# Three padding tiles in a decoder layer on one core, so that every large tile starts on a multiple of 512 bytes

## The chip, the cores and the metric

The kernel runs on one core of a Trainium2 chip. The metric is the device time of one execution in microseconds; several executions of the same program give a median. Its profile comes from one more execution, whose span (first to last instruction) and own time are given separately.

## The reference, cut to what matters

One layer of a decoder over 512 positions of width 2048, all in float32:

```
h    = rmsnorm(x) ;  proj = h @ w_in                    # 2048 -> 4608 columns
o_a  = sliding-window attention, 16 heads on 4 kv heads, window 128, q/k normalised, relative bias, sinks
o_b  = stick-breaking attention, 16 heads (scan of log(1 - sigmoid) from the right), strictly causal
x    = x + concat(rmsnorm(o_a), rmsnorm(o_b)) @ w_out   # 2048 -> 2048
h    = rmsnorm(x)
x    = x + square(relu(h @ w_up)) @ w_down              # 2048 -> 8192 -> 2048
```

## The kernel before

**Numbers as pairs.** Every large matrix product is made of three matmuls: each operand is split into a high part (a cast on ScalarE, L89) and a low part (the difference, on VectorE, L90), and high x high, high x low and low x high are added up in one bank of PSUM. So a tile that is needed for a product comes as `hi_...` and `lo_...`, or as `h2h` and `h2l`.

**Stages.** First come the input's transposes and the projections (`ps_kv`, `ps_qa`, `ps_v`, `ps_qk`), with the attention's small matmuls pumped in between: nine groups of 192 matmuls with 512 columns each. Here the moving or the stationary operand is `hT`, the transposed input (pools `big0` and `big1`), the other one a chunk of weights (pool `whl`). Then the two branches go through the output projection (`ps_o`, L114 to L116 in `mm3`): eight groups of 96 matmuls, stationary `ohl` (pools `big0`, `big1`), moving `hi_o` and `lo_o` (pool `whl`).

The up-projection (`ps_u`, L792 to L794) multiplies by a Winograd-like form of a 2 x 2 block product with seven products in place of eight. It runs over 32 groups g of 256 columns, and in each over 8 steps k: 21 matmuls of 256 columns, stationary `hi_u` and `lo_u` (pool `whl`), moving `h2h` and `h2l` of step k. These stay in SBUF for the whole stage, in pools of their own: `h2_0` to `h2_5` on the right side, `h2_6` and `h2_7` on the left. For each pair of steps GpSimd makes four sums of weights (`s_u`, L769, pool `sp`); ScalarE and VectorE split raw weights and sums (L89, L90). The group before is finished meanwhile, piece by piece (`u_finish`), with `al` (L827) as VectorE's last and longest piece, and its results go to DRAM (`ac`).

The down-projection (`ps_d`, L1023 to L1025) has the same seven-product form over 8 chunks and 2 halves: 2688 matmuls of 512 columns, stationary the stored activations `ad` (pool `ab`, on the right), moving `hi_d` and `lo_d` (pool `whl`). GpSimd makes the sums of weights (`T`, L918), VectorE adds each product to sums that stay in SBUF (`U`, `C`, pool `acc`, L962), and the last chunk brings scale, residual (`x2r`, L948) and the store.

**Order.** Each engine works through its instructions in the order in which the program names them. Loads and stores are issued on SP's queue, a few small ones on ScalarE's.

**Where the tiles lie.** Pools are stacked in each partition of SBUF, from the left (low addresses, upwards) and from the right (high addresses, downwards), and each tile is rounded up to 32 bytes. On the left stand 1,024 bytes of scratch, four constants of 32 bytes and the pool `const` with 1,792 bytes, so that `wst` and `whl` begin at 2,944 = 5 x 512 + 384. They take 16,384 and 32,768 bytes. Behind them `sm` has 28 small slots, 896 bytes, so that the next pool begins at 52,992 = 103 x 512 + 256. The right stack begins at 229,344 = 447 x 512 + 480 and goes down. All the larger tiles are multiples of 512 bytes long and keep their pool's remainder:

| pools | side | tiles | bytes past a multiple of 512, before | after |
|---|---|---|---|---|
| `wst`, `whl` | left | weights, raw and split (`hi_...`, `lo_...`) | 384 | 0 |
| `big1`, `big0`; later `h2_6`, `h2_7`, `ew`, `acc`, `x2p` | left | `hT`, `ohl`; `h2` of k = 6, 7; `a`, `ah`, `al`; `U`, `C`; `x2r` | 256 | 0 |
| `once`, `qkp`, `vp`, `wtp`, `wk`; later `h2_0` to `h2_5`, `sp`, `xw`; later `rw`, `t3`, `ab` | right | attention's tiles, `S`; `h2` of k = 0 to 5, `s_u`, `xs`; `st_d`, `T`, `ad` | 480 | 0 |

480 is 32 bytes off a multiple of 64; 384 and 256 are multiples of 128.

Of the kernel before, what the change touches and what calls it, by code (L numbers as in the profile page):

```python
# [12 lines left out]
F32 = mybir.dt.float32  # L13
# [7 lines left out]
P = 128  # L21
# [37 lines left out]
def hymba_layer(ctx: ExitStack, tc: tile.TileContext, x, norm_attn_g, w_in, q_norm_g, k_norm_g,  # L59
# [7 lines left out]
    const = ctx.enter_context(tc.tile_pool(name="const", bufs=1))  # L67
# [3 lines left out]
    sm = ctx.enter_context(tc.tile_pool(name="sm", bufs=4))  # L71
# [3 lines left out]
    odd, even, attn = ExitStack(), ExitStack(), ExitStack()  # L75
    big = {1: odd.enter_context(tc.tile_pool(name="big1", bufs=KD // 2)),
           0: even.enter_context(tc.tile_pool(name="big0", bufs=KD // 2))}
    once = attn.enter_context(tc.tile_pool(name="once", bufs=1, side="right"))
    qkp = attn.enter_context(tc.tile_pool(name="qkp", bufs=7, side="right"))
    vp = attn.enter_context(tc.tile_pool(name="vp", bufs=8, side="right"))  # L80
# [278 lines left out]
        return o  # L359

    oscr = dram.tile([2 * 8, P, T], F32, name="oscr")
    S = [once.tile([P, T], F32, name=f"S{b}") for b in range(2)]

    def finish_o(av, branch, c, keep=False):

        if c == 0:
            nc.scalar.square(out=S[branch], in_=av)
        else:
            sq = wk.tile([P, T], F32, tag="we", name=f"osq{branch}_{c}")
            nc.scalar.square(out=sq, in_=av)  # L370
            nc.gpsimd.tensor_tensor(out=S[branch], in0=S[branch], in1=sq, op=ALU.add)
        if keep:
# [257 lines left out]
    def branch_scale(b):  # L630
        ps = bank(f"rs{b}")
        for t in range(NT):
            nc.tensor.matmul(ps[:, 2 * t:2 * t + 2], S[b][:, t * P:(t + 1) * P], ones2, start=True, stop=True)
        r = const.tile([P, NT], F32, name=f"rb{b}")
# [345 lines left out]
    for cj in range(2 * NC):  # L980
# [10 lines left out]
        for s, (name, ai, _, b, more) in enumerate(D_PRODUCTS):  # L991
# [19 lines left out]
            if not more:  # L1011
                pool, tag = ((pa, "pa"), (pp, "pp"))[b // 2]
# [46 lines left out]
```

## Time and profile before

| | |
|---|---|
| time before, median of 3 runs (lowest, highest) | 2077.21 us (2077.02, 2078.11) |
| the profiled execution: own time, span | 2076.19 us, 2074.5 us |
| granted TensorE clock, mean | 0.996 |
| TensorE matmuls, busy | 2019.0 us, 97% (11652) |
| VectorE, busy | 1678.5 us, 81% |
| GpSimd, busy | 1045.7 us, 50% |
| ScalarE, busy | 1008.1 us, 49% |
| DMA | 350.28 MB, mean 169 GB/s |

In the rows PE is TensorE, PEld its weight load, DVE VectorE, ACT ScalarE, POOL GpSimd and SP the queue of the loads. A matmul's own duration in the trace overlaps with the next one's, because matmuls are pipelined; TensorE's pace is the distance from one matmul's start to the next one's. Idle time is put down to the instruction that ended it ("<-").

### The profile page before, as it was taken

What the parts mean: (1) busy time and instruction counts of PE and PEld (TensorE: products, weight loads), DVE (VectorE), ACT (ScalarE), POOL (GpSimd) and SP (SyncE); (2) the same over time, 40 slices, a digit from 0 to 9 for tenths busy, and PEclk for the clock granted to TensorE, in tenths of its full rate; (3) what the DMA queues carried; (4) which work ended last, traced back from release to release, by engine and by line L of the source; (5) the groups of instructions that cost most, each with busy time, mean ns of one, the idle gap of its engine ahead of it and who ended that gap; (6) DMA issues with size and microseconds to landing.
All of it is one profiled execution on the core that took longest, in us unless ns stands there. A gap on an engine that the chain in (4) does not pass through costs nothing. (4 is left out here: it accounts for less than half of the span.)

```text
span 2074.5 us, 30963 instructions
## 1 busy us (share of the span) xinstructions
PE 2019.0 (97%) x11652; PEld 1722.1 (83%) x11652; DVE 1678.5 (81%) x2038; ACT 1008.1 (49%) x1692; POOL 1045.7 (50%) x904
## 2 busy tenths in 40 slices
PE   8999999999999999999999999998999999999998
PEld 7777777777677889999999999997788888888876
DVE  4468646565775579999999999998889888988999
ACT  6267534544553565555555555554543333333332
POOL 0013322222220137777778787877755555555663
PEclk9999999999999999999999999999999999999999
DMA  6742332223345535656555555658756456456453
GB/s 217 116 133 82 102 96 73 72 92 117 103 140 175 180 109 163 195 186 194 187 188 194 185 196 184 198 183 326 265 208 230 158 206 244 144 204 260 152 187 108
DMA packets 213913, 350.28 MB, mean 169 GB/s; under 512 B 9779, under 2 KB 154372, under 8 KB 206596
## 3 DMA queue, kind: packets, MB, share of 16 engines
q1 hardware_dynamic: 211216, 345.02, 49.1%
q10 hardware_dynamic: 2548, 3.30, 1.4%
q8 instruction: 91, 1.49, 0.3%
q14 instruction: 58, 0.48, 0.1%
HBM read 270.16 MB, written 78.12 MB: 168 GB/s over the span
## 5 line engine op out<-in xcount | busy, mean ns | idle before, releaser
L794 PE MATMUL ps_u<-h2h,lo_u 128*128 128x256 f32 x1792 | 506.7, 283 | 15.7 <-DVE lo_u L90 15.7
L793 PE MATMUL ps_u<-h2l,hi_u 128*128 128x256 f32 x1792 | 506.4, 283 | 2.7 <-DVE h2l L90 2.7
L792 PE MATMUL ps_u<-h2h,hi_u 128*128 128x256 f32 x1792 | 506.3, 283 | 0.6 <-ACT h2h L89 0.6
L769 POOL TENSOR_TENSOR s_u<-st_u 128x256 f32<-128x256 f32 x256 | 254.6, 1015 | 242.3 <-DVE lo_u L90 171.7
L1024 PE MATMUL ps_d<-lo_d,ad 128*128 128x512 f32 x896 | 357.1, 399 | 6.4 <-DVE lo_d L90 6.4
L1023 PE MATMUL ps_d<-hi_d,ad 128*128 128x512 f32 x896 | 356.5, 398 | 6.5 <-DMA ad<-ac 4.9
L794 PEld LDWEIGHTS ps_u<-h2h,lo_u 128*128 128x128 f32 x1792 | 340.1, 190 | 21.9 <-DVE lo_u L90 21.8
L1025 PE MATMUL ps_d<-hi_d,ad 128*128 128x512 f32 x896 | 356.5, 398 | 0.0
L793 PEld LDWEIGHTS ps_u<-h2l,hi_u 128*128 128x128 f32 x1792 | 337.0, 188 | 3.2 <-DVE h2l L90 3.1
L792 PEld LDWEIGHTS ps_u<-h2h,hi_u 128*128 128x128 f32 x1792 | 336.6, 188 | 1.0 <-ACT h2h L89 1.0
L90 DVE TENSOR_TENSOR lo_d<-T,hi_d 128x1024 fp32r<-128x1024 f32 x128 | 244.8, 1924 | 49.4 <-ACT hi_d L89 49.4
L89 ACT CAST hi_u<-s_u 128x512 fp32r<-128x512 f32 x256 | 158.3, 618 | 226.4 <-POOL s_u L769 226.4
L918 POOL TENSOR_TENSOR T<-st_d,T 128x1024 f32<-128x1024 f32 x64 | 162.6, 2543 | 208.9 <-DVE lo_d L90 207.7
L90 DVE TENSOR_TENSOR lo_u<-s_u,hi_u 128x512 fp32r<-128x512 f32 x256 | 248.0, 969 | 8.6 <-ACT hi_u L89 8.4
L89 ACT CAST hi_d<-T 128x1024 fp32r<-128x1024 f32 x128 | 134.3, 1051 | 214.0 <-PE ps_d L1025 196.8
L1024 PEld LDWEIGHTS ps_d<-lo_d,ad 128*128 128x128 f32 x896 | 169.4, 189 | 49.9 <-DVE lo_d L90 8.9
L1023 PEld LDWEIGHTS ps_d<-hi_d,ad 128*128 128x128 f32 x896 | 169.6, 189 | 48.8 <-ACT a L816 4.9
L90 DVE TENSOR_TENSOR lo_u<-st_u,hi_u 128x384 fp32r<-128x384 f32 x256 | 202.3, 790 | 4.6 <-ACT hi_u L89 4.6
L1025 PEld LDWEIGHTS ps_d<-hi_d,ad 128*128 128x128 f32 x896 | 169.6, 189 | 41.1
L90 DVE TENSOR_TENSOR lo_d<-st_d,hi_d 128x1024 fp32r<-128x1024 f32 x96 | 190.1, 1996 | 13.3 <-ACT hi_d L89 13.2
L89 ACT CAST hi_d<-st_d 128x1024 fp32r<-128x1024 f32 x96 | 100.9, 1051 | 163.5 <-PE ps_d L1025 163.5
L769 POOL TENSOR_TENSOR s_u<-s_u,st_u 128x256 f32<-128x256 f32 x128 | 140.5, 1098 | 0.0
(220 smaller groups left out, 3823.6 us busy)
## 6 DMA issues: line engine op xcount, KB each, us to landing
st_u<-in_w_up SPq DMA_DIRECT2D x128, 512.0 KB, 4.4
st_d<-in_w_down SPq DMA_DIRECT2D x64, 1024.0 KB, 6.1
ad<-ac SPq DMA_DIRECT2D x56, 1024.0 KB, 6.4
ac<-ah SPq DMA_DIRECT2D x32, 896.0 KB
ac<-al SPq DMA_DIRECT2D x32, 896.0 KB, 4.8
st_qk<-in_w_in SPq DMA_DIRECT2D x64, 256.0 KB, 3.0
st_o<-in_w_out SPq DMA_DIRECT2D x32, 512.0 KB, 4.2
st_qa<-in_w_in SPq DMA_DIRECT2D x16, 512.0 KB, 3.8
```

The source lines that it names most:

```text
L89: nc.scalar.copy(out=hi, in_=st)
L90: nc.vector.tensor_tensor(out=lo, in0=st, in1=hi.bitcast(F32), op=ALU.subtract)
L769: nc.gpsimd.tensor_tensor(out=o, in0=a, in1=b, op=op)
L792: nc.tensor.matmul(o, wh[:, a], hh[:, b], start=first, stop=False, skip_group_check=True)
L793: nc.tensor.matmul(o, wh[:, a], hl[:, b], start=False, stop=False, skip_group_check=True)
L794: nc.tensor.matmul(o, wl[:, a], hh[:, b], start=False, stop=(k == KP - 1), skip_group_check=True)
L918: nc.gpsimd.tensor_tensor(out=o, in0=raw[cj, a, h], in1=raw[cj, b, h], op=ALU.subtract)
L1023: nc.tensor.matmul(o, al, bh[:, kk], start=first, stop=False, skip_group_check=True)
L1024: nc.tensor.matmul(o, al, bl[:, kk], start=False, stop=False, skip_group_check=True)
L1025: nc.tensor.matmul(o, ar, bh[:, kk], start=False, stop=end, skip_group_check=True)
```

## The change

Three tiles are allocated that nothing writes or reads: 480 bytes at the top of the right stack, in a pool of their own that is opened ahead of the others; 128 bytes at the end of `const`; 128 bytes in `sm`. 2,944 + 128 = 3,072 = 6 x 512; 52,992 + 256 = 53,248 = 104 x 512; 229,344 - 480 = 228,864 = 447 x 512. Everything else is as before.

```
@@ -75,6 +75,8 @@
     odd, even, attn = ExitStack(), ExitStack(), ExitStack()
     big = {1: odd.enter_context(tc.tile_pool(name="big1", bufs=KD // 2)),
            0: even.enter_context(tc.tile_pool(name="big0", bufs=KD // 2))}
+    edge = ctx.enter_context(tc.tile_pool(name="edge", bufs=1, side="right"))
+    edge.tile([P, 120], F32, name="pad_right")
     once = attn.enter_context(tc.tile_pool(name="once", bufs=1, side="right"))
     qkp = attn.enter_context(tc.tile_pool(name="qkp", bufs=7, side="right"))
     vp = attn.enter_context(tc.tile_pool(name="vp", bufs=8, side="right"))
@@ -359,6 +361,8 @@
         return o
 
     oscr = dram.tile([2 * 8, P, T], F32, name="oscr")
+    const.tile([P, 32], F32, name="pad_left")
+    sm.tile([P, 32], F32, tag="pad", bufs=1, name="pad_small")
     S = [once.tile([P, T], F32, name=f"S{b}") for b in range(2)]
```

## Rows read from the trace of the kernel before

**Rows 1.** Busy time of each engine by stage: window, PE, PEld, DVE, ACT, POOL, clock, DMA.

```profile
0.00:748.00 748.00, 728.37 (x3572) 565.72 (x3573) 455.25 (x782) 381.44 (x796) 160.75 (x264) 1.00 0.41 121
748.00:1422.80 674.80, 655.70 (x5394) 648.52 (x5392) 643.14 (x805) 378.47 (x651) 508.62 (x501) 1.00 0.57 185
1427.40:2074.50 647.10, 634.97 (x2688) 507.83 (x2688) 577.92 (x448) 245.96 (x244) 374.01 (x138) 0.99 0.56 206
```

**Rows 2.** Who waited for whom, 800 to 1400 us: us in total, times, longest.

```profile
ACT hi_u L89 <- POOL s_u L769: 208.0, 57, 5.1
POOL s_u L769 <- DVE lo_u L90: 129.6, 58, 3.0
...
PE ps_u L794 <- DVE lo_u L90: 14.3, 29, 0.8
DVE a L818 <- ACT a L816: 14.0, 29, 0.5
DVE lo_u L90 <- ACT hi_u L89: 7.6, 28, 0.3
```

**Rows 3.** Timeline of VectorE in up: start and duration in us.

```profile
1020.18 2.56 DVE L827 TENSOR_TENSOR al<-a,ah 128x1792 fp32r<-128x1792 f32 x1
...
1041.03 2.56 DVE L827 TENSOR_TENSOR al<-a,ah 128x1792 fp32r<-128x1792 f32 x1
```

**Rows 4.** Busy time in the steady part of down, columns as in the first group.

```profile
1500.00:2000.00 500.00, 500.00 (x2135) 401.94 (x2134) 443.44 (x353) 190.42 (x184) 279.02 (x102) 1.00 0.56 207
```

**Rows 5.** Who waited for whom, 1460 to 2020 us, longest in total.

```profile
ACT hi_d L89 <- PE ps_d L1025: 328.5, 192, 1.8
```

**Rows 6.** The chain that ended last, in order of time: start, us, what.

```profile
1458.48 0.50 PE ps_d L1023
...
2001.11 0.25 PE ps_d L1025
...
2030.53 0.50 PE ps_d L1024
```

**Rows 7.** Timeline of TensorE, one group of up: first of k = 0, first and last of k = 6.

```profile
1004.40 0.28 PE L792 MATMUL ps_u<-h2h,hi_u 128*128 128x256 f32 x1
...
1019.52 0.28 PE L792 MATMUL ps_u<-h2h,hi_u 128*128 128x256 f32 x1
...
1021.89 0.28 PE L794 MATMUL ps_u<-h2h,lo_u 128*128 128x256 f32 x1
```

**Rows 8.** Timeline of TensorE in down: two matmuls, 2134 intervals apart.

```profile
1500.04 0.39 PE L1023 MATMUL ps_d<-hi_d,ad 128*128 128x512 f32 x1
...
2000.01 0.40 PE L1024 MATMUL ps_d<-lo_d,ad 128*128 128x512 f32 x1
```

**Rows 9.** Timeline of TensorE in the branch outputs: two matmuls, 122 intervals apart.

```profile
657.07 0.39 PE L115 MATMUL ps_o<-lo_o,ohl 128*128 128x512 f32 x1
...
685.41 0.39 PE L116 MATMUL ps_o<-hi_o,ohl 128*128 128x512 f32 x1
```

**Rows 10.** Timeline of TensorE in the first projections: two matmuls, 155 intervals apart.

```profile
73.09 0.40 PE L114 MATMUL ps_qa<-hT,hi_qa 128*128 128x512 f32 x1
...
109.26 0.40 PE L116 MATMUL ps_qa<-hT,lo_qa 128*128 128x512 f32 x1
```

**Rows 11.** Instructions of single tiles: duration in ns, min/median/max, first and last start.

```profile
L827 DVE TENSOR_TENSOR al<-a,ah x32: 2024/2559/2565, 793.0 to 1438.4; 128x1792 fp32r<-128x1792 f32 x32
L90 DVE TENSOR_TENSOR h2l<-hq,h2h x8: 2025/2026/2336, 691.4 to 771.4; 128x1792 fp32r<-128x1792 f32 x8
L371 POOL TENSOR_TENSOR S<-S,osq x14: 1273/1289/1296, 193.9 to 640.6; 128x512 f32<-128x512 f32 x14
L973 POOL TENSOR_TENSOR C<-C,U x12: 1286/1745/2282, 2010.7 to 2061.5; 128x512 f32<-128x512 f32 x12
```

**Rows 12.** DMA issues: count, KB each, median us to landing.

```profile
x2r<-x2scr SPq DMA_DIRECT2D x16, 256.0 KB, 3.2
xs<-in_x SPq DMA_DIRECT2D x16, 256.0 KB, 3.1
```

More of the change, by code (lines that the diff above doesn't have):

```diff
@@ L77, in hymba_layer @@
            0: even.enter_context(tc.tile_pool(name="big0", bufs=KD // 2))}
+    edge = ctx.enter_context(tc.tile_pool(name="edge", bufs=1, side="right"))
+    edge.tile([P, 120], F32, name="pad_right")
     once = attn.enter_context(tc.tile_pool(name="once", bufs=1, side="right"))
@@ L361, in hymba_layer @@
     oscr = dram.tile([2 * 8, P, T], F32, name="oscr")
+    const.tile([P, 32], F32, name="pad_left")
+    sm.tile([P, 32], F32, tag="pad", bufs=1, name="pad_small")
     S = [once.tile([P, T], F32, name=f"S{b}") for b in range(2)]
```

## The prediction

> **What bounds the kernel now.** I read the page, then the stages, then who waits for whom in each, and last the starts of single matmuls. The profiled execution took 2076.19 us around its span of 2074.5; the median of the runs shown, 2077.21, is 1.0 above it, so the sum below is made against the profiled execution and carried over to the median as a difference. TensorE is busy 97% of the span, so the first question is in which stage its pace is the time. [rows 1] cuts the span into everything up to the branch outputs, the up-projection ("up") and the down-projection ("down").
>
> In up, 674.8 us, TensorE is busy 655.7 and VectorE 643.1 [rows 1], and the waits between 800 and 1400 us decide [rows 2]: ScalarE waits for GpSimd, GpSimd for VectorE, VectorE a little for ScalarE, nobody for TensorE. TensorE itself waits for VectorE's `lo_u`, 14.3 us in 29 groups, 0.5 us a group. The period shows it, too: `al` starts at 1020.18 and at 1041.03, 20.85 us apart [rows 3]. So up runs at VectorE's period, and TensorE has half a microsecond a group to spare.
>
> Down is the other way round. From 1500 to 2000 us TensorE is busy all of 500.00 us and VectorE 443.44 [rows 4], and between 1460 and 2020 ScalarE alone waits 328.5 us for TensorE, the top line of that view, in which TensorE waits for nobody [rows 5]. The chain that ended last is matmuls from 1458.48 to 2001.11, mostly VectorE up to 2030.53, then both in turn [rows 6]. At least 543 us of down thus go at TensorE's own pace.
>
> **What TensorE's pace is.** Here the starts are to be compared with the offsets of the tiles in the table further up.
> - Up, one group [rows 7]. The moving operand is `h2` of step k. For k = 0 to 5 it lies 480 bytes past a multiple of 512: 126 intervals from 1004.40 to 1019.52, 120.0 ns each. For k = 6, 256 bytes past: 20 intervals from there to 1021.89, 118.5 to 119. This group stands for 29, the fourth on, in which the starts give 120.03 and 118.89. The stationary operand and the neighbours are the same, and the granted clock of up is 1.00 [rows 1], the 2.4 GHz level; the step comes where k goes from 5 to 6. That is 1% for a moving operand at 480.
> - Down [rows 8]: stationary operand at 480, moving at 384. 2134 intervals between matmuls of 512 columns from 1500.04 to 2000.01, 234.29 ns each.
> - Branch outputs [rows 9], with the same roles: stationary `ohl` at 256, moving `hi_o` and `lo_o` at 384. 122 intervals from 657.07 to 685.41, 232.30 ns.
> - First projections [rows 10]: moving `hT` at 256, stationary at 384. 155 intervals from 73.09 to 109.26, 233.35 ns. Before up I found stretches of both paces, 232.3 and 233.4; 234.29 stands in down alone.
>
> So the trace has a price for an operand at 480, which is 32 bytes off a multiple of 64, where 256 and 384 are on one: 1.1 ns for a matmul of 256 columns, 0.9 to 2.0 for one of 512.
>
> **The change part by part.** The three tiles are neither written nor read: no instruction, DMA or wait of theirs is added, and no queue's order changes. What moves is addresses.
> - *Down, the stationary operand from 480 to 0.* In 543 us at 234.29 ns stand 2316 matmuls. Nearest row: the branch outputs, for the same roles. 2316 x (234.29 - 232.30) = 4.6 us gained; with the pace of [rows 10] 2316 x 0.94 = 2.2; if it isn't the offset, 0. I take 4.6, because the roles are the same and the step in up speaks for the offset. VectorE then has 443.4 us of work in 496 and stays under.
> - *Up, the moving operand from 480 to 0.* 126 x 1.14 = 0.14 us a group that TensorE comes earlier to its stop; there it waits 0.14 us longer for `lo_u`, as the period is VectorE's. Cost 0. If that cover were gone (VectorE much quicker), 32 x 0.14 = 4.6 us would be gained.
> - *Everything before up: from 256 and 384 to 0.* By the loops these are 2496 matmuls of 512 columns (nine projection groups of 192 and eight output groups of 96). No row shows an operand at a multiple of 512. 232.30 and 233.35 both occur already; I take 0, with a bound of 2496 x 1.05 = 2.6 us either way, and wider ones among the rivals.
> - *VectorE and GpSimd,* which set up's period. Their quickest instructions are equal at 256 and at 480 [rows 11]: 1792 columns on VectorE take 2024 ns (`al`, 256) and 2025 (`h2l`, six of eight at 480), 512 columns on GpSimd 1286 (`C`, 256) and 1273 (`S`, 480). ScalarE's casts I put at 0 with them. The bound is that 1% of GpSimd's or VectorE's share of up were moved: no more than 674.8 x 0.01 = 6.7 us, and 0.05% by VectorE's rows, 0.3 us. I take 0.
> - *DMAs.* 256 KB land in 3.2 us at 256 (`x2r`) and in 3.1 at 480 (`xs`) [rows 12], and neither in up nor in the steady part of down does TensorE wait for one [rows 2, 5]. 0; should `ad` land later than now, down would stop at the start of a product, which it doesn't do today.
> - *Reuse of space.* The left pools go up by 128 or 256 bytes and the right ones down by 480, so `xw` touches one tile more of `big0`, and `ew` and `acc` one more of `xw`. All of these had their last use before the new pool was opened. 0; a wait that came in all the same would stand once, ahead of the first tile of the pool.
>
> The Trainium skill ("SBUF — State Buffer", section "SBUF: two separate sides") has a rule that speaks against the change: SBUF's cachelines are 16 bytes. Every tile starts on a multiple of 32 already, so by that rule the padding would gain nothing and the time stay at 2077.2, against 2072.6 by the rows. The step in up doesn't agree with it [rows 7].
>
> Sum: -4.6 in down, 0 elsewhere. Profiled execution 2076.2 - 4.6 = 2071.6; median 2077.2 - 4.6 = **2072.6 us**, 0.22% faster.
>
> **The rivals.**
> 1. *Down settles at the slower of the two paces,* 233.35: -2.2, **2075**. For it: [rows 10] holds that pace for 155 matmuls with nothing at 480. Against it: the roles there are exchanged.
> 2. *The offset isn't the cause.* k = 0 to 5 differ from 6 and 7 in the stack, too (right and left), and `ad` is and stays on the right. Then nothing happens: **2077**. Against it: k = 0 to 5 lie all over the right stack and go at one pace.
> 3. *Every step up to 512 counts,* so that 256 and 384 are slow as well. At 1.99 ns an operand: 2 x 1.99 x 2496 = 9.9 us before up, 4.6 for the moving operand in down, 4.6 as above: -19.1, **2058**; half of it is 2067.6. Against it: 256 and 384 exchange their roles between [rows 9] and [rows 10], and no pace belongs to one of them.
> 4. *Slower: both operands at one offset get in each other's way.* Today moving and stationary differ by 96 or 128 bytes modulo 512; afterwards by 0. Priced by the one step that the trace has, 1% or 2.3 ns of 512 columns, in the 2496 matmuls before up: +5.7 us with nothing gained in down, **2083**; in down as well, 2316 x 2.3 = 5.3 more. It decides from 4.6 us / 2496 = 1.8 ns a matmul. Up would not notice: 168 x 1.1 = 0.2 us a group of the 0.5 spare. Nothing in the trace speaks for it or against it, as no pair of operands lies at one offset.
>
> **How the numbers follow.** Forecast 0.42; rivals 0.14, 0.17, 0.13, 0.14. 0.2% is 4.15 us, about what a measurement of this kernel can tell from no change; that line, 2073.05, is close to the forecast. Faster: three quarters of the forecast and all of rival 3, 0.44. Slower: most of rival 4 and a little of rival 2, 0.14. The rest is within 0.2%: 0.42. The forecast's own range is 2070 to 2075. For 8 in 10 it runs from 2063 (three quarters of rival 3) to 2081 (two thirds of rival 4).
>
> **What would show it.** Right: matmuls of down 232.3 ns apart between 1500 and 2000; k = 0 to 5 of up at 118.9 like k = 6, with the wait for `lo_u` 0.14 us longer and `al` still 20.85 apart; paces before up between 232.3 and 233.4; up ending when it did, down some 5 us earlier. Wrong: down still at 234.29 (rival 2), a pace under 232 before up (rival 3) or over 234 there (rival 4), or a period of up that moved, which would mean that VectorE or GpSimd feel the addresses after all.

## The result and the profile after

The changed kernel takes 2051.19 us (median of 4 runs, 2050.44 to 2052.35), the kernel before 2077.66 beside it (4 runs, 2077.02 to 2078.21). The ratio is 0.9873, 95% interval 0.9856 to 0.989: 26.5 us or 1.3% faster. The prediction was 2072.6 us with a range of 2063 to 2081, so the time lies far outside it, on the faster side. The profiled execution took 2051.57 us around a span of 2049.8, 24.7 us under the span before, with the same 30963 instructions and a mean granted clock of 0.995.

First the stages of the changed kernel (window, busy time of PE, PEld, DVE, ACT and POOL, granted clock, DMA share and GB/s); the last row is the steady part of down.

```profile
0.00:740.50 740.50, 720.47 (x3571) 565.63 (x3572) 454.35 (x782) 381.09 (x796) 161.34 (x264) 1.00 0.41 122
740.50:1415.70 675.20, 656.93 (x5394) 650.15 (x5393) 643.70 (x805) 378.61 (x651) 509.10 (x501) 1.00 0.57 185
1420.80:2049.80 629.00, 615.96 (x2688) 506.34 (x2688) 589.60 (x448) 246.51 (x244) 377.33 (x139) 0.99 0.57 211
...
1500.00:1990.00 490.00, 490.00 (x2164) 405.73 (x2163) 460.62 (x359) 191.52 (x183) 288.37 (x106) 1.00 0.55 206
```

Against [rows 1]: everything before up ends at 740.5 instead of 748.0, up lasts 675.2 instead of 674.8, and down with its tail 629.0 instead of 647.1. VectorE's work in up is the same, 643.70 for 643.14. In the steady part of down TensorE is busy without a gap, as in [rows 4], and gets through 2164 matmuls in 490 us where it had 2135 in 500. So 18 us come out of down, 7.5 out of what precedes up, and nothing out of up. No instruction is missing or new; the question is TensorE's pace.

Down, TensorE's timeline of the changed kernel (start and duration in us): two matmuls, 2162 intervals apart.

```profile
1500.17 0.39 PE L1029 MATMUL ps_d<-hi_d,ad 128*128 128x512 f32 x1
...
1990.22 0.39 PE L1028 MATMUL ps_d<-lo_d,ad 128*128 128x512 f32 x1
```

490.05 us / 2162 = 226.67 ns, where [rows 8] give 234.29 and the best pace of [rows 9] was 232.30. At the granted clock of 1.00, which is the 2.4 GHz level, 226.67 ns are 544 cycles, 512 columns and 32 more. The branch outputs have it as well, 120 intervals between these two rows, 226.75 ns each (the first of them are a little longer).

```profile
651.90 0.39 PE L116 MATMUL ps_o<-hi_o,ohl 128*128 128x512 f32 x1
...
679.11 0.39 PE L118 MATMUL ps_o<-hi_o,ohl 128*128 128x512 f32 x1
```

The same steady pace stands in the projections: 226.7 instead of the 232.3 and 233.4 of before. If all 2496 matmuls before up had gained 5.6 ns, that would be 14.0 us, and 7.5 are there. The difference is where the attention's small matmuls are pumped in. After such a block the large matmuls don't have the quick pace at once; here the second `ps_v` after one, and a later one of the same run.

```profile
161.18 0.40 PE L117 MATMUL ps_v<-lo_v,hT 128*128 128x512 f32 x1
161.42 0.40 PE L118 MATMUL ps_v<-hi_v,hT 128*128 128x512 f32 x1
...
162.35 0.39 PE L116 MATMUL ps_v<-hi_v,hT 128*128 128x512 f32 x1
162.58 0.40 PE L117 MATMUL ps_v<-lo_v,hT 128*128 128x512 f32 x1
```

0.24 us from one to the next at first, 0.23 later, and the next block comes soon. Averaged over the whole stretch ahead of up, the second to the eleventh distance after a block are 230.5 ns in the changed kernel, and those from the twelfth on 226.8. Over all intervals under 300 ns from a large matmul to whatever TensorE does next ahead of up (2290 before, 2293 after) the mean falls from 232.6 to 228.8 ns; 2290 x 3.8 = 8.7 us, near the 7.5 by which the stage is shorter.

Up keeps its period, as predicted. Its waits between 800 and 1380 us (us in total, times, longest), to be read beside [rows 2]:

```profile
ACT hi_u L91 <- POOL s_u L773: 203.1, 55, 5.2
POOL s_u L773 <- DVE lo_u L92: 124.9, 56, 3.0
...
PE ps_u L798 <- DVE lo_u L92: 12.7, 28, 0.7
```

TensorE still stops for `lo_u` in every group, 0.45 us a time for 0.49 before (the prediction had this wait grow by 0.14 us), and VectorE's `al` still comes 20.85 us apart, like [rows 3]:

```profile
1013.12 2.56 DVE L831 TENSOR_TENSOR al<-a,ah 128x1792 fp32r<-128x1792 f32 x1
...
1033.97 2.56 DVE L831 TENSOR_TENSOR al<-a,ah 128x1792 fp32r<-128x1792 f32 x1
```

Within a group, though, there is something that the forecast had the other way round. TensorE's timeline of one group in the changed kernel: 124 intervals within k = 0 to 5, then 19 within k = 6.

```profile
997.49 0.28 PE L797 MATMUL ps_u<-h2l,hi_u 128*128 128x256 f32 x1
...
1012.37 0.28 PE L798 MATMUL ps_u<-h2h,lo_u 128*128 128x256 f32 x1
...
1012.61 0.28 PE L797 MATMUL ps_u<-h2l,hi_u 128*128 128x256 f32 x1
...
1014.89 0.28 PE L798 MATMUL ps_u<-h2h,lo_u 128*128 128x256 f32 x1
```

Both stretches go at 120.0 ns. In [rows 7] k = 6 went at 118.9; it has become slower, and k = 0 to 5 no faster. VectorE feels none of it; the quickest `al` and `h2l` take 2024 ns, as in [rows 11] (tile, duration min/median/max in ns, first and last start):

```profile
L831 DVE TENSOR_TENSOR al<-a,ah x32: 2024/2561/2567, 785.9 to 1431.8; 128x1792 fp32r<-128x1792 f32 x32
...
L92 DVE TENSOR_TENSOR h2l<-hq,h2h x8: 2024/2026/2420, 685.1 to 764.2; 128x1792 fp32r<-128x1792 f32 x8
```

### The profile page after: what moved, and what is told of

Read it like the earlier page. It is cut to its first block, busy times and chain, and to the rows that moved or that the text cites. A ratio compares the mean times of both kernels' runs of the same rounds, so it can differ in the third digit from the quotient of the medians.

```text
span 2049.8 us, 30963 instructions
## 1 busy us (share of the span) xinstructions
PE 1993.6 (97%) x11652; PEld 1722.2 (84%) x11652; DVE 1690.3 (82%) x2038; ACT 1008.6 (49%) x1692; POOL 1050.0 (51%) x904
## 5 line engine op out<-in xcount | busy, mean ns | idle before, releaser
L798 PEld LDWEIGHTS ps_u<-h2h,lo_u 128*128 128x128 f32 x1792 | 344.4, 192 | 20.6 <-DVE lo_u L92 20.5
L1028 PE MATMUL ps_d<-lo_d,ad 128*128 128x512 f32 x896 | 351.1, 392 | 7.3 <-DVE lo_d L92 7.2
L1027 PE MATMUL ps_d<-hi_d,ad 128*128 128x512 f32 x896 | 350.3, 391 | 6.7 <-DMA ad<-ac 5.1
L1029 PE MATMUL ps_d<-hi_d,ad 128*128 128x512 f32 x896 | 349.9, 391 | 0.0
L797 PEld LDWEIGHTS ps_u<-h2l,hi_u 128*128 128x128 f32 x1792 | 344.5, 192 | 3.4 <-DVE h2l L92 3.4
L796 PEld LDWEIGHTS ps_u<-h2h,hi_u 128*128 128x128 f32 x1792 | 344.2, 192 | 1.1 <-ACT h2h L91 1.0
L92 DVE TENSOR_TENSOR lo_d<-T,hi_d 128x1024 fp32r<-128x1024 f32 x128 | 250.4, 1969 | 26.1 <-ACT hi_d L91 25.1
L92 DVE TENSOR_TENSOR lo_d<-st_d,hi_d 128x1024 fp32r<-128x1024 f32 x96 | 197.3, 2070 | 6.8 <-ACT hi_d L91 6.8
```

The lines of the kernel that those rows point to most:

```text
L92: nc.vector.tensor_tensor(out=lo, in0=st, in1=hi.bitcast(F32), op=ALU.subtract)
L796: nc.tensor.matmul(o, wh[:, a], hh[:, b], start=first, stop=False, skip_group_check=True)
L797: nc.tensor.matmul(o, wh[:, a], hl[:, b], start=False, stop=False, skip_group_check=True)
L798: nc.tensor.matmul(o, wl[:, a], hh[:, b], start=False, stop=(k == KP - 1), skip_group_check=True)
L1027: nc.tensor.matmul(o, al, bh[:, kk], start=first, stop=False, skip_group_check=True)
L1028: nc.tensor.matmul(o, al, bl[:, kk], start=False, stop=False, skip_group_check=True)
```

## The experiments

**The theories.** A: each operand has its own price, by its own offset (the prediction's reasoning, and its third rival with every step up to 512 bytes). B: what counts is how the two operands of one matmul lie to each other (the pairing of the fourth rival, with the sign turned round). In the expectations T1 and T2 are forms of A in which one operand alone decides, T4 and M want each operand on a multiple of 512 or of 256, and T3 and D are B. Below, X is the offset of the weights' pools `wst` and `whl`, Y that of `big0`, `big1` and the later left pools, Z that of the right stack, each in bytes past a multiple of 512. Before they are 384, 256 and 480, after 0, 0 and 0. Before up the operands lie at X and Y, in down at Z (stationary) and X (moving), in up at X (stationary) and Z (moving; Y for k = 6 and 7).

### The right stack alone

X, Y, Z = 384, 256, 0. Only the pad on the right is kept:

```
+    edge = ctx.enter_context(tc.tile_pool(name="edge", bufs=1, side="right"))
+    edge.tile([P, 120], F32, name="pad_right")
```

> Only the 480 bytes on the right: right tiles at 0, `wst`/`whl` at 384, `big0`/`big1` at 256. Down has its stationary operand at 0 and its moving one at 384. If the stationary operand's own start decides (T1): down goes at 226.7 ns a matmul, everything before up stays at 232.3 to 233.4, time about 2059 us. If the moving operand's start decides (T2), or both have to start at one offset (T3), or both at 0 (T4): down stays at 232 or more, time 2072 to 2077. Up keeps its period of 20.85 us in every theory, as VectorE sets it.

Measured: 2072.18 us (10 runs), ratio 0.9979 (0.9969 to 0.9989). Down, 2152 intervals:

```profile
1500.05 0.39 PE L1027 MATMUL ps_d<-hi_d,ad 128*128 128x512 f32 x1
...
2000.13 0.39 PE L1025 MATMUL ps_d<-hi_d,ad 128*128 128x512 f32 x1
```

232.38 ns. This is what the prediction priced, the stationary operand of down from 480 to 0, and it gives 4.5 us for the 4.6 predicted. So the size of the term fits this part, though the run doesn't show that the 480 was the reason: the difference to the moving operand went from 96 to 128 with it, which is that of the branch outputs in [rows 9]. The rest comes from the left side or from both together.

### The left side alone

X, Y, Z = 0, 0, 480:

```
+    const.tile([P, 32], F32, name="pad_left")
+    sm.tile([P, 32], F32, tag="pad", bufs=1, name="pad_small")
```

> Only the two paddings on the left: `whl` and `big0`/`big1` at 0, right tiles at 480. Everything before up has both operands at 0: 226.7 ns in all theories, about 7 us gained. Down has its stationary operand at 480, its moving one at 0. T1 (stationary decides), T3 (one offset), T4 (both at 0): down stays at 232 to 234.3, time about 2070. T2 (moving decides): down at 226.7, time about 2051.

Measured: 2069.57 us (5 runs), ratio 0.9967 (0.9954 to 0.998). The steady pace before up is 226.7 ns, although the attention's tiles, which the other engines work on there, still lie at 480, so that their offset doesn't stand in the way of this pace. Down, 2143 intervals:

```profile
1500.17 0.39 PE L1026 MATMUL ps_d<-lo_d,ad 128*128 128x512 f32 x1
...
2000.20 0.40 PE L1027 MATMUL ps_d<-hi_d,ad 128*128 128x512 f32 x1
```

233.33 ns. In down one pad alone gives 1.9 ns (right) or 1.0 (left), both give 7.6: it isn't a sum over operands, against theory A. The two kernels' gains against before, 4.5 and 7.1 us, add up to 11.6 of the 26.5. One group of up in this kernel says it more plainly, again 124 intervals of k = 0 to 5 and 19 of k = 6:

```profile
999.81 0.28 PE L795 MATMUL ps_u<-h2l,hi_u 128*128 128x256 f32 x1
...
1014.48 0.28 PE L796 MATMUL ps_u<-h2h,lo_u 128*128 128x256 f32 x1
...
1014.72 0.28 PE L795 MATMUL ps_u<-h2l,hi_u 128*128 128x256 f32 x1
...
1017.00 0.28 PE L796 MATMUL ps_u<-h2h,lo_u 128*128 128x256 f32 x1
```

118.3 ns for k = 0 to 5, whose moving operand still lies at 480, and 120.0 for k = 6, where nothing lies at 480. The step of [rows 7], on which the prediction built its price of 480, has turned round.

### Equal offsets, other than a multiple of 512

Four kernels put the operands at offsets that are equal, or 256 apart, by the sizes of the three pads alone (bytes on the left, in `sm`, on the right):

```
roles:    128, 384, 224   ->  X, Y, Z =   0, 256, 256
all_256:  384, 128, 224   ->  X, Y, Z = 256, 256, 256
all_480:   96, 128, none  ->  X, Y, Z = 480, 480, 480
all_128:  256, 128, 352   ->  X, Y, Z = 128, 128, 128
```

> `wst`/`whl` at 0, everything else at 256. T1 (stationary decides): `ps_kv`, `ps_qa`, `ps_qk` (stationary `whl`) at 226.7, `ps_o` and down (stationary at 256) at 232 or more; about 2072. T2 (moving decides): the reverse, `ps_o` and down at 226.7, `ps_qk` at 232 or more; about 2055. T3 (one offset) and T4 (both at 0): 232 or more everywhere, about 2073. If a multiple of 256 is enough for both operands (modulus 256 in place of 512): 226.7 everywhere, 2051.

> All large tiles at 256 bytes past a multiple of 512. T3 (the two operands have to start at one offset, whichever): 226.7 ns everywhere, 2051. T1, T2, T4 with multiples of 512: 232 or more everywhere, 2072 to 2077. With multiples of 256: 226.7, 2051; `roles` tells that from T3.

> All large tiles at 480 bytes past a multiple of 512, where the kernel before has its right stack. Two theories are left. Each operand has to start at a multiple of 256 by itself (M): then both are off here, down stays at 232 to 235 ns, everything before up too, about 2075 us. Or the two operands of a matmul have to start at one remainder of 256, whichever it is (D): 226.7 ns before up and in down, about 2051.

> All large tiles at 128 past a multiple of 512. M (multiples of 256, each operand): 232 or more, about 2075. D (one remainder of 256 for both): 226.7, about 2051. If multiples of 128 are enough when both are on one: 226.7 as well; `fine` tells that from D.

Measured, one run each: 2051.78, 2052.49, 2058.88 and 2051.79 us. Down in the first (2161 intervals), the third (2206) and the fourth (2162):

```profile
1500.18 0.39 PE L1028 MATMUL ps_d<-lo_d,ad 128*128 128x512 f32 x1
...
1990.01 0.39 PE L1029 MATMUL ps_d<-hi_d,ad 128*128 128x512 f32 x1
```

```profile
1500.06 0.39 PE L1025 MATMUL ps_d<-hi_d,ad 128*128 128x512 f32 x1
...
2000.08 0.39 PE L1026 MATMUL ps_d<-lo_d,ad 128*128 128x512 f32 x1
```

```profile
1500.08 0.39 PE L1028 MATMUL ps_d<-lo_d,ad 128*128 128x512 f32 x1
...
1990.13 0.39 PE L1027 MATMUL ps_d<-hi_d,ad 128*128 128x512 f32 x1
```

226.67, 226.66 and 226.67 ns (`all_256`: 226.67, too), and 226.67 before up in all four. Both operands at 480, 32 bytes off any multiple of 64, go as fast as both at 0: theory A is gone, and so is its form with 512 bytes as the good place. A difference of 256 is as good as none (`roles`), one of 128 is not ([rows 9], `right_only`): as far as tried, the effect repeats every 256 bytes, and not every 128.

### Small differences

X, Y, Z = 0, 128, 64 (pads of 128, 256 and 416 bytes), to see whether a difference of 64 is still bad:

> `whl` at 0, `big0`/`big1` at 128, right tiles at 64. M: one operand of every pair is off, so 232 or more everywhere, about 2073. D: the remainders differ in every pair (by 128 before up, by 64 in down), so the same. If it is enough that the difference is a multiple of 64 or of 32: 226.7 everywhere, 2051; but right_only showed 232.4 in down at a difference of 128, so that is not expected. Between the pairs: if a difference of 64 costs as much as one of 128, down goes at 232.4 like right_only; if the size of the difference counts, at something else.

Measured: 2079.05 us (one run; before 2076.33 beside it). Down, 2143 intervals:

```profile
1500.12 0.39 PE L1029 MATMUL ps_d<-hi_d,ad 128*128 128x512 f32 x1
...
2000.15 0.40 PE L1027 MATMUL ps_d<-hi_d,ad 128*128 128x512 f32 x1
```

233.33 ns, with every tile on a multiple of 64. Before up, at a difference of 128, 232.4. All the pads of the change are there, in other sizes, and nothing is gained. That down's 1.0 ns a matmul doesn't show in this one run goes with a granted clock of 0.94 from 1430 to 1500 us, where the kernel before had 0.97, and with an up stage that is 1.9 us longer.

All kernels so far in one table, ordered by the difference of the two operands' starts modulo 256 (taken the shorter way round):

| difference | 512 columns, ns | from | 256 columns (up), ns | from |
|---|---|---|---|---|
| 0 | 226.67 | after, left_only before up, roles, all_256, all_480, all_128 | 120.00 | the same kernels (left_only: k = 6) |
| 32 | 233.33 | left_only, down | 118.33 | left_only, k = 0 to 5 |
| 64 | 233.33 | fine, down | 117.77 | fine, k = 0 to 5 |
| 96 | 234.29 | before, down | 120.0 | before, k = 0 to 5 |
| 128 | 232.3 to 233.4 | before, right_only and fine before up; right_only, down | 118.4 to 118.9; in right_only 118.7 or 120.0 | before and fine, k = 6; right_only |

With 512 columns equal starts are best by 5.6 to 7.6 ns. With 256 columns they are, beside 96, the worst, by 1.1 to 2.2 ns.

The steps of 1 to 2 ns among the unequal rows should not be read as a law. The table leaves out which operand lies higher, and in up the two have exchanged their roles, so that 32, 64 and 96 stand for opposite signs in the two halves. And one pair of addresses can go at two paces: in `right_only` k = 0 to 5 go at 118.7 ns in 23 of the 31 groups from the second on and at 120.0 in the other 8, and the branch outputs of [rows 9], 232.30 ns there, go at 233.3 in `no_al_before` (further down), which is the same kernel up to that place:

```profile
656.05 0.39 PE L115 MATMUL ps_o<-lo_o,ohl 128*128 128x512 f32 x1
...
684.51 0.39 PE L116 MATMUL ps_o<-hi_o,ohl 128*128 128x512 f32 x1
```

Here, too, 122 intervals. The 233.35 of [rows 10], on which the prediction's first rival rests, is such a second pace: in `right_only`, with the same offsets there, the same stretch goes at 232.4.

### Both at 480 again

`all_480` has the quick pace everywhere and is yet 7.7 us over the changed kernel. The same kernel, timed:

> The same kernel as all_480, which had the pace of 226.7 ns everywhere but lost 6 us before up, with a wait of 1.9 us in the first projections and the granted clock at its lower level right behind it. If that was one execution: 2051 now. If tiles at 480 cost elsewhere: 2058 again.

Measured: 2055.25 us (2 runs), ratio 0.9895 (0.9875 to 0.9915). It stays some 4 us over the changed kernel. The time is lost ahead of up, whose first matmul comes at 747.1 and 744.2 us in its two profiles and at 740.8 in the changed kernel's. In `all_480`, from 95 to 112 us, TensorE waits once for VectorE to take a product out of PSUM (`f_q`), and ScalarE for a load of weights:

```profile
ACT hi_qa L103 <- DMA st_qa<-in_w_in: 17.6, 2, 16.0
...
PE ps_qa L114 <- DVE f_q L317: 1.9, 1, 1.9
```

In the changed kernel the load is waited for less long, and the second line isn't there:

```profile
ACT hi_qa L105 <- DMA st_qa<-in_w_in: 14.8, 2, 14.4
```

The longest wait for that load is 15.8 to 16.7 us in four profiles with the right stack at 480 (before, `left_only`, `all_480` twice) and 14.1 to 15.0 in the six so far with it at 0, 64, 128 or 256. But a fifth profile with it at 480 (`no_al_before`, below) has no such wait, 0.3 us in all. After the stop of 1.9 us the granted clock falls for a while; `all_480` and the changed kernel, 100 to 120 us, columns as in the first fence:

```profile
100.00:120.00 20.00, 18.07 (x73) 14.49 (x72) 10.17 (x16) 9.34 (x17) 0.00 (x0) 0.91 0.66 215
```

```profile
100.00:120.00 20.00, 20.00 (x88) 16.05 (x87) 13.08 (x21) 13.94 (x25) 0.21 (x1) 1.00 0.61 198
```

73 matmuls for 88, at a mean clock of 0.91 for 1.00. In the second profile of this kernel the stop is 1.0 us and the clock of the same window 1.00, with 82 matmuls. Whether the load is late because of the 480 is not shown: no run isolates it, and the fifth profile speaks against it.

### What up pays once VectorE doesn't hide it

In up the pace can't show in the time, because VectorE sets the period. Two kernels leave out `al` in 31 of the 32 groups, one at the offsets of before and one at those of after; a third is the second with `h2` moved to 64, by pads of 448 bytes (right) and 64 (left).

```
-        al = ew.tile([P, 7, HP], F32R, tag="al", name=f"al{g}")
+        if g == 0:
+            kept_al.append(ew.tile([P, 7, HP], F32R, tag="al", name="al"))
+        al = kept_al[0]
...
-        nc.vector.tensor_tensor(out=al, in0=a[:, 1:8], in1=ah.bitcast(F32), op=ALU.subtract)
+        if g == 0:
+            nc.vector.tensor_tensor(out=al, in0=a[:, 1:8], in1=ah.bitcast(F32), op=ALU.subtract)
```

> The kernel before, with the low part `al` of the activations computed for the first group alone and stored again for the others, which takes VectorE's longest instruction, 2.56 us, out of every group of up. If VectorE sets up's period and TensorE is next: the period falls from 20.85 to TensorE's own 126 x 120.03 + 42 x 118.89 = 20.1 us, 31 x 0.73 = 22 us gained, about 2054. If TensorE's half microsecond of waiting comes from elsewhere (GpSimd's sums): the period stays over 20.6 and less than 8 us are gained.

> The same edit in the changed kernel (`al` computed for the first group alone). TensorE's pace in up is 120.00 there, no better than before, so the period should be the same 168 x 0.12 = 20.16 us: 21 us gained, about 2030. If the change had made up's matmuls quicker and VectorE only hid it, the period would fall under 20.

> The kernel of no_al_after (changed kernel, `al` computed for the first group alone, so that TensorE sets up's period), with `h2` moved 64 bytes past a multiple of 512 for up alone, while `whl` stays at 0 and down gets its right tiles at 0 again. In `fine` this pair of operands had the quickest pace of up, 117.77 ns. If unequal starts really are the better ones for matmuls of 256 columns: period 168 x 117.77 = 19.79 us against 20.16, 31 x 0.37 = 11.6 us less than no_al_after, about 2022, with down unchanged at 226.7. If the pace in `fine` came from the stops in each group: 120.0, period 20.16, about 2034.

Measured, one run each: 2054.67, 2033.94 and 2020.49 us. The window from 800 to 1400 us of the first and the second, columns as above:

```profile
800.00:1400.00 600.00, 598.45 (x5003) 598.24 (x5001) 541.88 (x717) 358.84 (x592) 449.54 (x472) 1.00 0.62 200
```

```profile
800.00:1400.00 600.00, 596.35 (x4970) 596.14 (x4968) 538.44 (x712) 358.53 (x592) 447.29 (x468) 1.00 0.61 198
```

The third kernel's window reaches past the end of its up stage, so it goes by the period from group 10 to group 26, counted from 0. Their first matmuls in the third kernel:

```profile
946.97 0.28 PE L798 MATMUL ps_u<-h2h,hi_u 128*128 128x256 f32 x1
...
1263.55 0.28 PE L798 MATMUL ps_u<-h2h,hi_u 128*128 128x256 f32 x1
```

Over these 16 groups the periods are 20.100, 20.160 and 19.787 us. The second is 168 x 120.00 = 20.160 and the third 168 x 117.78 = 19.787: up at TensorE's pace to the nanosecond. In none of the three does TensorE stop for `lo_u` any more, and the cover is gone: the changed offsets then cost 0.06 us a group against before, 1.9 us in 32 groups, and 64 bytes between the operands give 0.37 us a group, 11.9 in all (the two times, one run each, differ by 13.45). So the pace of 256 columns is real and goes the other way from that of 512. Without `al` the gain of the change is 2054.67 - 2033.94 = 20.7 us for the 26.5 with it.

### Two tries to relieve VectorE in up

That invites to take work off VectorE. `al_two` gives two of the seven parts of `al` to GpSimd; `sums_ahead` gives GpSimd a third buffer for its sums, so that it can run ahead:

```
-        nc.vector.tensor_tensor(out=al, in0=a[:, 1:8], in1=ah.bitcast(F32), op=ALU.subtract)
+        nc.gpsimd.tensor_tensor(out=al[:, 0:2], in0=a[:, 1:3], in1=ah[:, 0:2].bitcast(F32), op=ALU.subtract)
+        nc.vector.tensor_tensor(out=al[:, 2:7], in0=a[:, 3:8], in1=ah[:, 2:7].bitcast(F32), op=ALU.subtract)
...
-    sp = mlp.enter_context(tc.tile_pool(name="sp", bufs=2, side="right"))
+    sp = mlp.enter_context(tc.tile_pool(name="sp", bufs=3, side="right"))
-        junk = xw.tile([P, 512], F32, tag="junk", bufs=2, name=f"j2{n}{t}")
+        junk = xw.tile([P, 512], F32, tag="junk", bufs=1, name=f"j2{n}{t}")
```

> The changed kernel, with two of the seven parts of `al` subtracted on GpSimd, five on VectorE. VectorE is relieved of about 0.7 us a group, which is what TensorE waits in each group. If GpSimd (76% busy) has room for 1.3 us more and the two don't block each other longer: the period falls to 20.2 to 20.5 us, 10 to 20 us gained on the changed kernel, about 2035. If GpSimd's sums come later by it: no gain or a loss.

> The changed kernel with three buffers in place of two for GpSimd's sums `s_u` (and one in place of two for a scratch tile of the branch outputs, for room). If VectorE's 0.27 us of idle time in each group, which ends with sums that come late, is the sums' buffer: up to 32 x 0.27 = 8.6 us gained on the changed kernel, about 2043. If VectorE's own work sets the period: no more than 2 us either way, 2051. If GpSimd, running ahead, blocks VectorE at worse places: slower, as in al_two.

Measured: `al_two` 2069.28 us (4 runs, ratio to before 0.9957, 0.994 to 0.9974), 18 us over the changed kernel. Its window from 800 to 1400 us:

```profile
800.00:1400.00 600.00, 571.42 (x4704) 565.75 (x4703) 578.18 (x702) 326.66 (x562) 520.38 (x477) 1.00 0.57 185
```

VectorE is as busy as in the changed kernel (577.74 there), with less to do; GpSimd has 520.38 for 461.66, the period is 21.41 us for 20.86, and the longest wait of TensorE for `lo_u` grew from 0.7 to 1.8 us. `sums_ahead`: 2052.86 us (4 runs, ratio 0.9881, 0.9865 to 0.9898), period 20.88, no better than the changed kernel. VectorE's subtractions show where the relief went (800 to 1380 us: busy us, mean ns, idle time before): first the changed kernel, then `al_two`, then `sums_ahead`.

```profile
L92 DVE TENSOR_TENSOR lo_u<-s_u,hi_u 128x512 fp32r<-128x512 f32 x223 | 217.4, 975 | 7.6 <-ACT hi_u L91 7.6
L92 DVE TENSOR_TENSOR lo_u<-st_u,hi_u 128x384 fp32r<-128x384 f32 x223 | 176.0, 789 | 0.0
```

```profile
L92 DVE TENSOR_TENSOR lo_u<-st_u,hi_u 128x384 fp32r<-128x384 f32 x217 | 200.4, 924 | 0.0
```

```profile
L92 DVE TENSOR_TENSOR lo_u<-s_u,hi_u 128x512 fp32r<-128x512 f32 x223 | 228.0, 1022 | 0.0
```

In `al_two` those of the raw weights take 924 ns for 789, more than the shorter `al` saves. In `sums_ahead` the idle time of 7.6 us is gone, but those of the sums take 1022 ns for 975, 10.5 us over 223 of them. No version tried that does the whole work is faster than the changed kernel.

## Why the prediction was wrong

**What bounds each stage:** right. Up stayed at VectorE's 20.85 us, its length moved by 0.4 us, and TensorE's pace there, which did change, cost nothing. Down went at TensorE's own pace and gave most of the gain. `al`, `h2l` and the loads of [rows 12] kept their durations.

**What TensorE's pace is:** here the prediction failed. It read k = 0 to 5 against k = 6 as a price of an operand at 480, its own offset alone. (Taken again from the trace, the starts give 119.97 and 118.84 ns for its 120.03 and 118.89; the price of 1.1 ns is the same.) Moved with it, and not considered, was the difference to the stationary operand: 96 for the one, 128 for the other. `left_only` tells the two readings apart (480 kept, difference 32: 118.3 ns), and `all_480` as well. Of the signs named for being right, down came at 226.67 ns in place of 232.3 and k = 0 to 5 stayed at 120.0 in place of 118.9; "a pace under 232 before up" had been named as a sign of being wrong, and came.

**Down, the stationary operand from 480 to 0:** the term was 2316 x 1.99 = 4.6 us, measured 18.1 by the stage's window, and 2316 x (234.29 - 226.67) = 17.6 by the pace. The step that failed is "Nearest row: the branch outputs, for the same roles", with 232.30 taken as the pace of well-placed operands. Those stood 128 bytes apart modulo 256 and were slow themselves; no pair of the large products in the kernel before had equal starts, so no steady stretch of its trace could show the quick pace (some of the attention's small ones had, with both operands on the right stack, but they come in short blocks). `right_only` is the change that the term described, and there its number holds, 232.38 ns and 4.5 us. That is partly luck, as the reason given, the 480, is refuted by `left_only` and `all_480`: the branch outputs were the right row because their difference is 128, too.

**Everything before up:** taken as 0 with a bound of 2.6 us, measured 7.5, for the same reason; the block-wise interruptions keep it from the 14.0 of a steady pace.

**The rivals.** The fourth asked the right question, what happens when both operands have one offset, and noted that no row could answer it; it gave that only the slower sign, at 2.3 ns, where the truth was 5.6 to 7.6 ns the other way. The third came nearest to the time (2058), for a reason that `all_480` and `all_128` refute. An unknown that no row of the trace bounds should have had both signs, and more than the nearest row's step as its size.

**The rule that spoke against the change.** By the Trainium skill's 16-byte cachelines ("SBUF — State Buffer", section "SBUF: two separate sides") nothing should have changed, as every tile was on a multiple of 32 before: the 26.5 us contradict that use of it. The Trainium skill, same page, section "Who interferes with whom", gives TensorE two independent read ports, one for the moving operand and one for weight loads, and says that it never waits on anyone. With equal starts it keeps 226.67 ns in down while VectorE is busy 460.62 of 490 us and GpSimd 288.37; but the runs show that its pace depends on how those two operands lie to each other, 226.67 ns against 232 to 234.

**What stays open:** what in the chip makes the period of 256 bytes; why 256 columns go the other way from 512; which other tile widths and types go which way; whether the sign of a difference counts, and why one difference can go at two paces; whether it is a matmul's own stationary operand that counts or the next one's, as all of a stage lie at one offset; and whether the later load of `st_qa` at 480 is the offset's doing.

## What to carry to other kernels

Where a stage goes at TensorE's own pace in matmuls of 512 columns, try starts of both operands that are equal modulo 256 bytes, by padding a pool, and measure the distance from start to start in a steady stretch: here it was 226.67 ns against 232 to 234. Where another engine sets the stage's period, as in up, such a pace is worth nothing, and for 256 columns equal starts were even the slower choice. The best pace in a trace isn't the floor: ask which arrangement of the operands the trace doesn't hold, and price it in both directions.

## What the runs showed of the hardware

- A matmul of 512 columns, back to back at the granted clock of 1.00, takes 226.67 ns (544 cycles at 2.4 GHz) with equal starts modulo 256 and 232.3 to 234.3 otherwise; one of 256 columns takes 120.00 ns (288 cycles) with equal starts and 117.8 to 120.0 otherwise.
- The absolute alignment of the two doesn't show in the pace: 0, 128, 256 and 480 bytes past a multiple of 512 gave the same 226.67.
- After a block of small matmuls the quick pace of the changed kernel came back only by and by: 230.5 ns on average over the second to the eleventh distance, 226.8 from the twelfth on.
- At a difference of 128 the same addresses went at 118.7 or 120.0 ns (256 columns), and at 232.3 or 233.3 (512).
- Two parts of seven of one subtraction, given to GpSimd, lengthened the period of VectorE and GpSimd from 20.86 to 21.41 us, and VectorE's subtractions of the raw weights from 789 to 924 ns.
